# A Strassen feed forward on one Trainium2 core: two sums of weights move from VectorE to GpSimd

## The chip, the cores and the metric

The kernel runs on one core of a Trainium2 chip. The metric is device microseconds of one execution; the comparison is made with the median of several runs. The engines are named as the profile names them: PE (TensorE, matrix products; PEld is its weight load), DVE (VectorE), ACT (ScalarE), POOL (GpSimd) and SP (SyncE, which issues most of the DMAs).

## The reference

The model is one encoder block in fp32 on 256 tokens of width 2048: two branches (a gated linear attention and a Hyena convolution), a merge, a LayerNorm, then the feed forward that this change touches and a second LayerNorm:

```python
h = _layernorm(DEEPNORM_ALPHA * h + mix, ln1_g[l], ln1_b[l])
ff = jnp.square(jax.nn.relu(h @ w_ff1[l])) @ w_ff2[l]      # 2048 -> 8192 -> 2048
h = _layernorm(DEEPNORM_ALPHA * h + ff, ln2_g[l], ln2_b[l])
```

## The kernel before

Every fp32 operand is split into a high and a low part (`cast` on ScalarE makes the high part, `rest` on VectorE subtracts it from the source). A product then takes three matmuls: high by high, high by low, low by high.

The feed forward is worked off in quarters of the 8192 hidden channels. The first quarter of the first matrix (`ff1_first`) runs alone. Then come 48 slots (`ff_pairs`, `SLOTS = 48`). Each slot does two things on TensorE: products of the second matrix for the quarter that is ready, and one block of 128 hidden channels of the first matrix for the next quarter (the f block, lines L147 and L151, summed in one PSUM buffer).

The products with the second matrix use a Strassen scheme (Winograd's form): a weight block of 128 x 2048 is four units a, b, c, d of 128 x 512, and seven products, each a unit or a sum of units by one of seven `forms` of the hidden activations, replace eight. The seven are taken in three parts: units a, b, c as they are (`plain_split`, pieces `b_h` and `b_l`), the two sums a+d and a+b+d (`pair_split`, pieces `whi` and `wlo` from `ring`), and the two sums b+d and a+b+c+d (`last_split`, pieces in `fa`). Their products are on lines L1245, L1246 and L1247 (`form_products`).

The raw block lies in one of three ring buffers (`ring_tile`), which SyncE fills two slots ahead (`ring_load`, L1150). Its four units are u[0] to u[3]. `plain_split` splits a, b, c, then makes the sums in place: u[0] = a+d and u[3] = a+d+b on VectorE. Two DMAs that accumulate, issued by GpSimd, make the others: u[1] = b+d by adding d from memory (L1170), and u[2] = c+a+b+d by adding u[3] (L1171).

Inside a slot the instructions on ScalarE, VectorE and TensorE keep the order in which the program writes them (`pin`, which holds the instruction in program order while `pinned[0]` is set):

1. TensorE: a, b, c of this slot, the two pair products, the f block, then the two last products of the slot before.
2. `plain_split` of the next slot, then the first half of the next f weights (`half_split`, tiles `fraw`).
3. `pair_split` of the next slot; every eighth slot, sums out of PSUM (`take_sums`, tiles `zr`).
4. In the slots that FORMED lists (10, 11, 13, 14, 16, 17, 19, 20 and so on by 16), `forms`: the seven forms of two hidden blocks. In the third round the forms are plain casts with one subtraction.
5. `quad_sum`, which empties the PSUM of the f block into `fr` (ScalarE copies one half to `f_l`, VectorE adds the other); the second half of the f weights; `last_split`. In the last slots, one step of the joins (L1271 to L1278).

Of the kernel before, what the change touches and what calls it, by code (L numbers as in the profile page):

```python
# [13 lines left out]
ALU = mybir.AluOpType  # L14
# [29 lines left out]
def block_kernel(  # L44
# [25 lines left out]
    nc = tc.nc  # L70
# [37 lines left out]
    def weight_half(n, h):  # L108
        return (wp.tile([P, D // 2], F32R, tag="whi", bufs=3, name=f"whi{n}_{h}"),
                wp.tile([P, D // 2], F32R, tag="wlo", bufs=3, name=f"wlo{n}_{h}"))  # L110
# [138 lines left out]
    with tc.tile_pool(name="xp", bufs=1) as xp, tc.tile_pool(name="xq", bufs=1) as xq:  # L249
        def units(pool, tag, n, **kw):  # L250
            t = pool.tile([P, n, OPENING * P], F32R, tag=tag, name=f"open_{tag}", **kw)
            return lambda a, b: t[:, a:b].rearrange("p k (b j) -> p k b j", b=OPENING)
# [41 lines left out]
        for k0, n in PIECES:  # L294
# [13 lines left out]
            if k0 == 0:  # L308
                hi, lo = places[0]
# [775 lines left out]
    def ring_tile(p):  # L1085
        m = p % 3
        if m not in ring:
            ring[m] = wp.tile([P, D], F32, tag="raw", bufs=3, name=f"ring{m}")
        return ring[m]
# [10 lines left out]
    def pin(ins):  # L1100
        return tc.keep_in_program_order(ins) if pinned[0] else ins

    def VT(dst, a, b, op):
        return pin(nc.vector.tensor_tensor(dst, a, b, op=op))  # L1104

    def cast(hi, src):
        return pin(nc.scalar.copy(hi, src))  # L1107

    def rest(lo, src, hi):
        return VT(lo, src, hi.bitcast(F32), ALU.subtract)  # L1110
# [46 lines left out]
    def plain_split(p):  # L1157
        raw, n = ring_tile(p), FF_PAIRS + 2 * p
        hi = ep.tile([P, D], F32R, tag="xh", name=f"b_h{p}")
        lo = ep.tile([P, 1024], F32R, tag="wx", name=f"b_l{p}")  # L1160
        u = units(raw)
        at = slice(0, 1024), slice(1024, 1536)
        low = lo, hi[:, 1536:2048]
        for c in at:
            cast(hi[:, c], raw[:, c])
        for c, dst in zip(at, low):
            rest(dst, raw[:, c], hi[:, c])
        VT(u[0], u[0], u[3], ALU.add)
        VT(u[3], u[0], u[1], ALU.add)
        nc.gpsimd.dma_start(u[1], wblk[n, :, 1536:2048], accum_op=ALU.add)  # L1170
        nc.gpsimd.dma_start(u[2], u[3], accum_op=ALU.add)  # L1171
        h = units(hi)
        pieces_of[p, 0] = list(zip(h[:3], units(lo) + h[3:]))

    def split_units(p, kind, hi, lo, raw):
        by_unit = [t.rearrange("p (u c) -> p u c", c=512) for t in (hi, lo)]
        cast(by_unit[0], raw)
        rest(by_unit[1], raw, by_unit[0])
        pieces_of[p, kind] = list(zip(units(hi), units(lo)))

    def raw_units(p):
        return ring_tile(p).rearrange("p (u c) -> p u c", c=512)

    def pair_split(p):
        hi, lo = weight_half(FF_PAIRS + 2 * p, 0)
        split_units(p, 1, hi, lo, raw_units(p)[:, 0:4:3])

    def last_split(p):
        fa_slot(4)
# [21 lines left out]
    def ff1_first():  # L1211
        begun = begin_three()
        for c2 in range(8):
            for c in range(2):
                if begun:
                    ps, parts, n = begun.pop(0)
                    finish_block(ps, hT, parts, n)
                else:
                    ps = channel_psum(f"f0_{c2}_{c}")
                    parts = next_block()  # L1220
                    for h in range(2):
                        channel_products(ps, hT, parts[h], range(8 * h, 8 * h + 8))
                quad_sum(c2, c, ps, f"f0_{c2}_l{c}")
                at = 2 * c2 + c
                if at in (12, 13):
                    block_load(at - 12)
                if at in (13, 14):
                    ring_load(at - 13)
                if at == 14:
                    plain_split(0)  # L1230
                    pair_split(0)
            sq = squares(c2)
            forms(c2)
            if 2 <= c2 < 6:
                zc = z1[:, 1, (c2 - 2) * 512:(c2 - 1) * 512]
                with tc.issue_after(sq.ins):
                    nc.vector.tensor_tensor(zc, zc, rows1[:, 1, (c2 - 2) * 512:(c2 - 1) * 512], op=ALU.add)
# [43 lines left out]
    def ff_pairs():  # L1281
        pss = [psum_side(f"w{j}") if j not in (2, 3, 4) else psum_main(f"w{j}") for j in range(7)]
        joins = []
        for s in range(SLOTS):
# [12 lines left out]
            if more:  # L1297
                plain_split(s + 1)
                half_split(s + 1, 0)
            take_sums(pss, s, (0, 1, 2))  # L1300
            if more:
                pair_split(s + 1)
# [266 lines left out]
```

## Time and profile before

| | us |
|---|---|
| median of 3 runs | 1796.89 (1796.34 to 1797.45) |
| the profiled execution | 1796.92 |
| its span | 1795.1 |
| PE busy | 1784.6 (99%) |
| DVE busy | 1453.9 (81%) |
| ACT busy | 1037.7 (58%) |
| POOL busy | 164.7 (9%) |

The span is the time between the first and the last event of the profiled execution. The busy time of an engine is the sum of its instructions' spans, without register, semaphore and DMA issuing instructions on most queues; DMA issues of GpSimd do count. The granted clock of TensorE is 1.00 in all windows of the stage. In a row of the timeline stand start, duration, engine, line, operation, output <- inputs, shape and count, and in brackets the idle time of the engine before it with the engine that ended it. VectorE's instructions overlap a little: the next one starts about 0.08 us before the one ahead has ended, so distances of starts are used for sums. The program's helpers `VT` and `rest` record all their instructions at L1104, `cast` at L1107; there one goes by the tile.

### The profile page before, as it was taken

Reading aid. Unit: us, or ns where it says so; the run is one execution under the profiler, and the core shown is the slowest. Engines: PE = TensorE matmul, PEld = TensorE weight load, DVE = VectorE, ACT = ScalarE, POOL = GpSimd, SP = SyncE. Lnnn points to the kernel's source line nnn. Section 1 sums busy time; section 2 is a strip of 40 time slices with the busy share of each in tenths; the row PEclk is TensorE's granted clock in tenths of the full one; section 3 lists DMA queues with packets and bytes.
Section 4 is the critical chain, followed back from the end, with each engine's and each line's share of the span. In section 5 each row is a group of like instructions: output and inputs, shape, how many; then the busy total and the mean of one; then the engine's idle time right before and its main releaser. Section 6 shows DMA issues by size and latency. Waiting matters only on the chain.

```text
span 1795.1 us, 23458 instructions
## 1 busy us (share of the span) xinstructions
PE 1784.6 (99%) x8787; PEld 1506.7 (84%) x8787; DVE 1453.9 (81%) x1869; ACT 1037.7 (58%) x1399; POOL 164.7 (9%) x217
## 2 busy tenths in 40 slices
PE   9999999999999999999999999999999999999998
PEld 7888888888888888888888889888888888888887
DVE  6789887875679998998845558688899999999867
ACT  6678667875344444444544445566666666666632
POOL 1011110000111101111000000001111111111100
PEclk9999999999999999999999999999999999999999
DMA  8668866445797979798555664658888878888763
GB/s 325 233 249 291 253 232 201 144 169 201 235 297 244 287 251 283 246 308 249 203 190 187 266 240 153 225 180 274 250 242 252 271 240 259 255 248 267 216 226 123
DMA packets 79281, 424.76 MB, mean 237 GB/s; under 512 B 9816, under 2 KB 12392, under 8 KB 38464
## 3 DMA queue, kind: packets, MB, share of 16 engines
q1 hardware_dynamic: 47808, 336.61, 50.8%
q0 software_dynamic: 24304, 66.99, 18.2%
q10 hardware_dynamic: 7056, 19.67, 3.1%
q8 instruction: 69, 1.13, 0.3%
q14 instruction: 44, 0.36, 0.1%
HBM read 381.86 MB, written 16.25 MB: 222 GB/s over the span
## 4 chain that ended last, share of the span: by engine, by line
PE 93%; DVE 3%; ACT 1%; DMA 1%; issue 1%; SPq 0%; DVEq 0%; POOL 0%; ACTq 0%
PE f L147 11%; PE f L151 6%; PE w L1246 4%; PE w L1247 4%; PE w L1245 4%; PE g L200 3%; PE g L199 3%; PE g L201 3%; PE ux L199 3%; PE ux L201 3%; PE ux L200 3%; PE k L147 2%; PE v L201 2%; PE v L200 2%; PE v L199 2%; PE ho L200 2%
## 5 line engine op out<-in xcount | busy, mean ns | idle before, releaser
L86 ACT CAST whi<-raw 128x1024 fp32r<-128x1024 f32 x392 | 412.6, 1054 | 408.0 <-PE ux L201 86.8
L87 DVE TENSOR_TENSOR wlo<-raw,whi 128x1024 fp32r<-128x1024 f32 x392 | 477.2, 1221 | 205.1 <-ACT whi L86 202.9
L147 PE MATMUL f<-hT,whi 128*128 128x512 f32 x984 | 242.8, 391 | 1.1 <-DVE fr L1104 1.1
L147 PEld LDWEIGHTS f<-hT,whi 128*128 128x128 f32 x984 | 180.8, 188 | 36.4 <-DVE fr L1104 1.5
L151 PEld LDWEIGHTS f<-hT,wlo 128*128 128x128 f32 x984 | 126.2, 191 | 4.8
L1104 DVE TENSOR_TENSOR wlo<-fraw,whi 128x1024 fp32r<-128x1024 f32 x96 | 117.2, 1220 | 13.3 <-ACT whi L1107 11.0
L151 PE MATMUL f<-hT,wlo 128*128 128x256 f32 x984 | 127.7, 283 | 0.0
L1107 ACT CAST whi<-ring 128x1024 fp32r<-128x1024 f32 x48 | 50.6, 1054 | 102.8 <-DVE ring L1104 98.4
L1170 POOL DMA_DIRECT2D ring<-wblk x48 | 41.7, 868 | 700.9 <-DVE ring L1104 700.9
L1107 ACT CAST whi<-fraw 128x1024 fp32r<-128x1024 f32 x96 | 100.9, 1051 | 0.1
L200 PE MATMUL g<-wlo,xT 128*128 128x512 f32 x256 | 100.2, 391 | 0.0
L201 PE MATMUL ux<-whi,xT 128*128 128x512 f32 x256 | 99.9, 390 | 0.0
L201 PE MATMUL g<-whi,xT 128*128 128x512 f32 x256 | 99.9, 390 | 0.0
L200 PE MATMUL ux<-wlo,xT 128*128 128x512 f32 x256 | 99.7, 389 | 0.0
L199 PE MATMUL g<-whi,xT 128*128 128x512 f32 x256 | 93.9, 392 | 0.0
L199 PE MATMUL ux<-whi,xT 128*128 128x512 f32 x256 | 89.7, 389 | 0.0
L1107 ACT CAST b_h<-ring 128x1024 fp32r<-128x1024 f32 x96 | 75.4, 834 | 22.5 <-PE w L1247 18.0
L1104 DVE TENSOR_TENSOR b_l<-ring,b_h 128x1024 fp32r<-128x1024 f32 x48 | 58.6, 1220 | 12.5 <-ACT b_h L1107 12.5
L1104 DVE TENSOR_TENSOR ring<-ring 128x512 f32<-128x512 f32 x96 | 65.9, 687 | 1.5
L1104 DVE TENSOR_TENSOR wlo<-ring,whi 128x1024 fp32r<-128x1024 f32 x48 | 58.8, 1224 | 1.9 <-ACT whi L1107 0.3
L1104 DVE TENSOR_TENSOR fa<-ring,fa 128x1024 fp32r<-128x1024 f32 x48 | 58.4, 1217 | 0.0
L1171 POOL DMA_DIRECT2D ring<-ring x48 | 58.1, 1210 | 0.0
(537 smaller groups left out, 4297.5 us busy)
## 6 DMA issues: line engine op xcount, KB each, us to landing
raw<-wblk SPq DMA_DIRECT2D x204, 1024.0 KB, 5.1
fraw<-wblk SPq DMA_DIRECT2D x48, 1024.0 KB, 4.8
ring<-wblk SPq DMA_DIRECT2D x48, 1024.0 KB, 7.3
Td<-T POOLq DMA_DIRECT2D x32, 384.0 KB, 5.6
conv_sb<-conv_rows SPq DMA_DIRECT2D x12, 1024.0 KB, 11.6
Tl<-Td POOLq DMA_DIRECT2D x16, 768.0 KB, 9.4
ring<-wblk POOLq DMA_DIRECT2D x48, 256.0 KB, 4.3
ring<-ring POOLq DMA_DIRECT2D x48, 256.0 KB, 5.1
```

What stands on the lines that cost most here:

```text
L86: return (nc.scalar.copy(hi, src), nc.vector.tensor_tensor(lo, src, hi.bitcast(F32), op=ALU.subtract))
L87: nc.vector.tensor_tensor(lo, src, hi.bitcast(F32), op=ALU.subtract))
L147: MM(ps[:, :, ts], hi[:, js], act[:, kt, :, ts], start=(kt == 0 and opens), stop=(kt == KT - 1))
L151: MM(ps[:, 0, ts], lo[:, js], act[:, kt, 0, ts], start=False, stop=False)
L199: MM(pss[tb], sh, wh, start=(kt == 0), stop=False)
L200: MM(pss[tb], sh, wl, start=False, stop=False)
L201: MM(pss[tb], sl, wh, start=False, stop=(kt == KT - 1))
L1104: return pin(nc.vector.tensor_tensor(dst, a, b, op=op))
L1107: return pin(nc.scalar.copy(hi, src))
L1245: pin(MM(ps, sh, wh, start=(i == 0), stop=False))
L1246: MM(ps, sh, wl, start=False, stop=False)
L1247: pin(MM(ps, sl, wh, start=False, stop=(i == 7)))
```

## The change

In `plain_split` both sums go from VectorE to GpSimd, and their places are exchanged: a+d now goes to u[3], and a+d+b to u[0]. The first sum then reads u[0] and u[3] and overwrites u[3], which no other instruction of `plain_split` reads; the second overwrites u[0], and so comes after the cast and the subtraction that read u[0]. The accumulating DMA takes u[0] in place of u[3], and `pair_split` reads the two units in the other order. GpSimd's two sums and its two DMA issues stand in this order in its queue.

```diff
@@ plain_split
         for c, dst in zip(at, low):
             rest(dst, raw[:, c], hi[:, c])
-        VT(u[0], u[0], u[3], ALU.add)
-        VT(u[3], u[0], u[1], ALU.add)
+        pin(nc.gpsimd.tensor_tensor(u[3], u[0], u[3], op=ALU.add))
+        pin(nc.gpsimd.tensor_tensor(u[0], u[3], u[1], op=ALU.add))
         nc.gpsimd.dma_start(u[1], wblk[n, :, 1536:2048], accum_op=ALU.add)
-        nc.gpsimd.dma_start(u[2], u[3], accum_op=ALU.add)
+        nc.gpsimd.dma_start(u[2], u[0], accum_op=ALU.add)
@@ pair_split
-        split_units(p, 1, hi, lo, raw_units(p)[:, 0:4:3])
+        split_units(p, 1, hi, lo, raw_units(p)[:, 3::-3])
```

## The prediction

> **What bounds the kernel now.** I read the page first, then the windows of the stage that the change touches, then what TensorE waits for there, then VectorE's order of work in two kinds of slot.
>
> ```profile
> span 1795.1 us, 23458 instructions
> PE 1784.6 (99%) x8787; PEld 1506.7 (84%) x8787; DVE 1453.9 (81%) x1869; ACT 1037.7 (58%) x1399; POOL 164.7 (9%) x217
> ```
>
> TensorE is busy for all but 10.5 us of the span; VectorE, from which work is taken, is busy for 81% of it. The share is an average, so I look at the stage: the 48 slots of the feed forward, from about 1195 to 1690 us. Window rows give TensorE's, its weight load's, VectorE's, ScalarE's and GpSimd's busy time in turn.
>
> ```profile
> 1190.00:1300.00 110.00, 110.00 (x577) 94.82 (x576) 91.88 (x107) 72.14 (x93) 17.38 (x20) 1.00 0.81 248
> 1300.00:1410.00 110.00, 110.00 (x562) 94.25 (x561) 101.52 (x133) 76.59 (x104) 17.79 (x21) 1.00 0.83 247
> ...
> 1480.00:1590.00 110.00, 108.89 (x562) 93.21 (x561) 103.80 (x138) 71.90 (x97) 17.58 (x20) 1.00 0.81 249
> 1590.00:1690.00 100.00, 99.36 (x506) 84.77 (x505) 90.74 (x107) 64.67 (x84) 17.56 (x20) 1.00 0.84 252
> ```
>
> TensorE has no gap at all in the first two rows and 1.11 and 0.64 us in the last two. The waits of TensorE in the whole stage (1190 to 1700 us; total, times, longest) name both:
>
> ```profile
> PE f L147 <- DVE fr L1104: 1.1, 1, 1.1
> PE w L1246 <- DVE wlo L1104: 0.6, 1, 0.6
> ```
>
> So relief of VectorE can win at most 1.1 + 0.6 = 1.7 us here, 0.1% of the time. About 0.2% (3.6 us) is what a measurement of this kernel can tell from no change. The same windows say how little room there is the other way: VectorE is busy 101.52 of 110 and 103.80 of 110 us in the stretches that hold most of the forms. The chain of waits before the one wait of 1.1 us runs over VectorE, through the sums themselves:
>
> ```profile
> 1546.61 0.60 DVE b_h L1104
> 1547.21 0.61 DVE ring L1104
> ...
> 1553.45 0.35 DVE fr L1104
> 1553.80 0.04 issue
> 1553.84 2.11 PE f L147 x8
> ```
>
> That wait is on `quad_sum`, which empties the one PSUM buffer left for the f block: its VectorE instruction must be through before TensorE opens the next f block.
>
> **The beat of a slot.** TensorE's beat is the distance of two such rows of the chain, 1420.27 - 1409.94 = 10.33 us:
>
> ```profile
> 1409.94 1.91 PE f L151 x16
> 1420.27 1.91 PE f L151 x16
> ```
>
> VectorE in a slot without forms (start, duration, operation, wait before it):
>
> ```profile
> 1232.34 1.22 DVE L1104 TENSOR_TENSOR b_l<-ring,b_h 128x1024 fp32r<-128x1024 f32 x1 [0.77 <-ACT b_h L1107]
> ...
> 1238.64 0.42 DVE L1104 TENSOR_TENSOR fr<-f,f_l 128x256 f32<-128x256 f32 x1 [0.75 <-ACT f_l L1107]
> 1239.59 1.23 DVE L1104 TENSOR_TENSOR wlo<-fraw,whi 128x1024 fp32r<-128x1024 f32 x1 [0.52 <-ACT whi L1107]
> ...
> 1242.71 1.22 DVE L1104 TENSOR_TENSOR b_l<-ring,b_h 128x1024 fp32r<-128x1024 f32 x1 [0.76 <-ACT b_h L1107]
> ```
>
> From b_l to b_l are 10.37 us, of which VectorE waits 0.75 + 0.52 + 0.76 = 2.03, so it needs 8.3 of TensorE's 10.33. A slot with forms:
>
> ```profile
> 1315.48 1.22 DVE L1104 TENSOR_TENSOR b_l<-ring,b_h 128x1024 fp32r<-128x1024 f32 x1
> 1316.62 0.68 DVE L1104 TENSOR_TENSOR b_h<-ring,b_h 128x512 fp32r<-128x512 f32 x1
> 1317.22 1.41 DVE L1104 TENSOR_TENSOR ring<-ring 128x512 f32<-128x512 f32 x2
> 1318.55 1.22 DVE L1104 TENSOR_TENSOR wlo<-fraw,whi 128x1024 fp32r<-128x1024 f32 x1
> ...
> 1322.39 0.69 DVE L1104 TENSOR_TENSOR fa<-fr,fa 128x512 fp32r<-128x512 f32 x1 [0.36 <-ACT fa L1107]
> 1323.00 0.55 DVE L1104 TENSOR_TENSOR fa<-fw,fa 128x384 fp32r<-128x384 f32 x1
> 1323.47 0.41 DVE L1104 TENSOR_TENSOR fr<-f,f_l 128x256 f32<-128x256 f32 x1
> 1324.02 1.23 DVE L1104 TENSOR_TENSOR wlo<-fraw,whi 128x1024 fp32r<-128x1024 f32 x1
> ...
> 1326.30 1.22 DVE L1104 TENSOR_TENSOR b_l<-ring,b_h 128x1024 fp32r<-128x1024 f32 x1
> ```
>
> Here b_l to b_l is 10.82 us, 0.49 over TensorE's beat, with one wait of 0.36. The `fr` instruction ends at 1323.88, and TensorE opens the f block here:
>
> ```profile
> 1325.36 1.07 PE L147 MATMUL f<-hT,whi 128*128 128x512 f32 x4
> ```
>
> So 1325.36 - 1323.88 = 1.5 us is the slack at this deadline. By the list FORMED in the code, full forms stand in slots 10, 11, 13, 14, 16, 17, 19, 20 and again 16 slots later: twice eleven slots with eight forms each. That the books close: the second group has 8 x 0.49 = 3.9 too much, its three other slots give back 3 x 2.03 = 6.1, the seven sums out of PSUM in slots 31 and 32 cost 7 x 0.6 = 4.2 (below, 1528.46 - 1526.66 = 1.8 for three); that leaves 2.0 against a slack of 1.5, and the trace has a wait of 1.1.
>
> ```profile
> 1526.66 1.88 DVE L1104 TENSOR_TENSOR zr<-zr,w 128x512 f32<-128x512 f32 x3
> 1528.46 1.22 DVE L1104 TENSOR_TENSOR wlo<-ring,whi 128x1024 fp32r<-128x1024 f32 x1
> ...
> 1617.23 0.68 DVE L1272 TENSOR_TENSOR zr<-zr 128x512 f32<-128x512 f32 x1
> ...
> 1645.35 0.69 DVE L1104 TENSOR_TENSOR fa<-fr,fa 128x512 fp32r<-128x512 f32 x1 [0.47 <-ACT fa L1107]
> ```
>
> The last two rows are a join (0.68 us, 0.6 start to start, as b_h above: 1317.22 - 1316.62) and one of the four small forms of slots 42 to 46 (0.6 and a wait of 0.47).
>
> **What the change removes.** On VectorE the two sums of each slot, 1318.55 - 1317.22 = 1.33 us start to start. These are the rows for what goes and for what GpSimd does already:
>
> ```profile
> L1104 DVE TENSOR_TENSOR ring<-ring 128x512 f32<-128x512 f32 x96 | 65.9, 687 | 1.5
> L1170 POOL DMA_DIRECT2D ring<-wblk x48 | 41.7, 868 | 700.9 <-DVE ring L1104 700.9
> L1171 POOL DMA_DIRECT2D ring<-ring x48 | 58.1, 1210 | 0.0
> ring<-wblk SPq DMA_DIRECT2D x48, 1024.0 KB, 7.3
> ring<-ring POOLq DMA_DIRECT2D x48, 256.0 KB, 5.1
> ```
>
> If nothing else happened, a forms slot would fall to 9.5 us of VectorE and both waits would go: 1796.9 - 1.7 = 1795.2. TensorE's and SyncE's instruction order stays as it was; ScalarE's and VectorE's differ by a few places in the opening.
>
> **What it adds.** 96 GpSimd instructions on 128x512 fp32. The trace has no arithmetic on GpSimd, so their price is bounded: 0.69 us, the same sum on VectorE, from below; 1.21 us, GpSimd's own longest row on a 128x512 piece of this buffer, is the row of the right engine, and I take it; twice that, 2.42, is my far end. GpSimd itself has room: 2 x 1.21 + 0.87 + 1.21 = 4.5 us of 10.33. In its queue the first sum stands ahead of the second and both ahead of the two DMA issues; the first waits for the raw block (issue to landing 7.3 us), the second for b_l, since it overwrites what b_l reads. Behind the second sum wait the DMAs and ScalarE's cast of the pair. The DMAs have cover: they land after 5.1 us and `last_split` reads them about a slot later. The set-up instruction that GpSimd gets in front of its first sum lies where it is idle, so I cost it at nothing:
>
> ```profile
> 1100.00:1180.00 80.00, 0.00 (x0) 1.00 0.47 171
> ```
>
> [...]
>
> **The open cost: do both engines read at once?** Nearly all VectorE instructions of this stage read two operands in SBUF, as the new sums do. No row shows GpSimd reading SBUF beside VectorE. The ends: no loss at all, or the engines take turns and VectorE loses each sum's whole duration. I take turns as the likelier. With them VectorE's beat changes by 2 x 1.21 - 1.33 = +1.09 us a slot: forms slots need 11.91 (1.58 over the beat), others 9.4 (0.9 under).
>
> - First group: 8 x 1.58 - 3 x 0.9 + 3 x 0.6 (three sums out of PSUM in slots 15 and 16) = 11.7, less slack 1.5: 10.2 us of TensorE waits.
> - Second: 12.6 - 2.7 + 4.2 = 14.1, less 1.5, less the 1.1 there now: 11.5.
> - Slots 39 to 47: nine times 0.9 under is -8.1, seven PSUM sums +4.2, eight joins of 0.6 +4.8, four small forms of about 1.07 +4.3: 5.2, less 1.5, less the 0.6 there now: 3.1.
>
> That is 24.8. In a forms slot GpSimd can run below the `fr` instruction (one operand from PSUM; 1324.02 - 1323.47 = 0.55 to the next start) and the wait of 0.36; taking 0.35 of that as used, 16 x 0.35 = 5.6 come off: +19.2 us, so 1796.92 + 19.2 = 1816. The profiled execution took 1796.92 us (span 1795.1), the median of the runs is 1796.89, so nothing needs correcting.
>
> [...]
>
> **Rivals.**
> 1. Side by side. Both engines run at full rate, VectorE falls to 9.5 us in forms slots, the second sum is ready 1.21 us after b_l, sooner than VectorE's two were (b_h lay between). The two waits go: 1795.2 us. For it: GpSimd is busy 17.38 of 110 us in the first window. Against it: nothing in the rows. It decides if VectorE's 1.22 us subtractions keep their duration.
> 2. GpSimd sets the beat. At 2.42 us a sum and turns, VectorE gains 3.51 a slot: forms slots 14.3 (4.0 over, 16 times: 64), the others 11.8 (1.5 over, 31 times: 46): about 1907 us. It needs the far end of the price.
> 3. Turns lost. The second sum finds VectorE already in the subtraction behind b_h and starts 1.14 us later (the distance of two 128x1024 starts, 1316.62 - 1315.48); ScalarE's cast of the pair and VectorE's next subtraction wait for it. In the 16 forms slots that is 18 us more, 1834; in the eight join slots too, 1843.
>
> **How the numbers follow.** Turns, with rival 3 as their upper part: 0.64, of which 0.04 ends within 0.2% because the sums cost nearer 0.69 (2 x 0.69 - 1.33 is 0.05, which changes nothing). Side by side: 0.28, of which 0.26 is no measurable change, since 1.7 us is under 3.6, and 0.02 a larger gain elsewhere. GpSimd as the bound: 0.06. Something that I don't see and that speeds it up: 0.02. The chance for turns is a judgement on an operation without a row; what the rows fix is that there is nearly nothing to win and that the forms slots have no room to lose. Range: from side by side (1795) to turns lost in all loaded slots (1843); the likeliest case alone is 1800 to 1843. Faster 0.04, same 0.30, slower 0.66.
>
> **What would show it.** If turns: VectorE's 1.22 us rows grow in some executions to about 2.4 or show idle time that GpSimd releases, and TensorE's waits at the f block (on `fr`) sum to some 20 us, in slots 10 to 20 and 26 to 36 and hardly elsewhere. If GpSimd's rows are near 1.2 us, the price holds; near 2.4, rival 2. If VectorE's durations don't move and its busy time falls by 66 us, side by side is right and the forecast is wrong. Waits of ScalarE's pair cast on GpSimd well over the 2.08 us that it waits for VectorE now would be rival 3:
>
> ```profile
> 1401.09 1.05 ACT L1107 CAST whi<-ring 128x1024 fp32r<-128x1024 f32 x1 [2.08 <-DVE ring L1104]
> ```

## The result, and the profile after

The change makes the kernel slower: 1810.99 us (median of 6 runs, 1809.1 to 1812.78) against 1797.12 us (1796.34 to 1797.45), a ratio of 1.0079 with a 95% interval of 1.0069 to 1.0089. The forecast was 1816 us, slower. The profiled execution is the fastest of the six: 1809.1 us, with a span of 1807.3 us, 12.2 us over that of before. From the page of the changed kernel:

```profile
span 1807.3 us, 23439 instructions
PE 1789.6 (99%) x8787; PEld 1506.7 (83%) x8787; DVE 1477.6 (82%) x1773; ACT 1038.5 (57%) x1399; POOL 321.4 (18%) x313
```

VectorE has 96 instructions fewer and yet 23.7 us more busy time (1477.6 after, 1453.9 before). The groups of the changed kernel say which instructions grew (count, busy time in all, mean ns of one, idle time before them):

```profile
L1104 DVE TENSOR_TENSOR wlo<-fraw,whi 128x1024 fp32r<-128x1024 f32 x96 | 176.9, 1843 | 11.0 <-ACT whi L1107 9.6
L1168 POOL TENSOR_TENSOR ring<-ring 128x512 f32<-128x512 f32 x48 | 77.3, 1611 | 371.0 <-DMA ring<-wblk 363.4
L1169 POOL TENSOR_TENSOR ring<-ring 128x512 f32<-128x512 f32 x48 | 80.2, 1671 | 168.9 <-DVE b_l L1104 168.9
```

VectorE's subtraction `wlo<-fraw` took 1220 ns on average before and takes 1843 now; its operands and shape are the same. VectorE's order in the forms slot that the prediction showed, one slot from b_l to b_l:

```profile
1317.10 1.21 DVE L1104 TENSOR_TENSOR b_l<-ring,b_h 128x1024 fp32r<-128x1024 f32 x1
1318.23 0.68 DVE L1104 TENSOR_TENSOR b_h<-ring,b_h 128x512 fp32r<-128x512 f32 x1
1318.83 2.31 DVE L1104 TENSOR_TENSOR wlo<-fraw,whi 128x1024 fp32r<-128x1024 f32 x1
1321.18 1.23 DVE L1104 TENSOR_TENSOR wlo<-ring,whi 128x1024 fp32r<-128x1024 f32 x1
...
1324.84 0.42 DVE L1104 TENSOR_TENSOR fr<-f,f_l 128x256 f32<-128x256 f32 x1
1325.39 1.77 DVE L1104 TENSOR_TENSOR wlo<-fraw,whi 128x1024 fp32r<-128x1024 f32 x1
...
1328.22 1.21 DVE L1104 TENSOR_TENSOR b_l<-ring,b_h 128x1024 fp32r<-128x1024 f32 x1
```

and GpSimd's two sums in the same slot (the bracket is its idle time and what ended it):

```profile
1318.44 1.62 POOL L1169 TENSOR_TENSOR ring<-ring 128x512 f32<-128x512 f32 x1 [3.49 <-DVE b_l L1104]
...
1324.46 1.61 POOL L1168 TENSOR_TENSOR ring<-ring 128x512 f32<-128x512 f32 x1 [2.33 <-DMA ring<-wblk]
```

Read the two together. GpSimd's second sum is released by b_l at 1318.44, while VectorE is in b_h; b_h ends at 1318.91, the sum at 1320.06. VectorE's next subtraction is in its row from 1318.83, but it ends at 1321.14, 1.08 us after the sum, and has taken 2.31 - 1.22 = 1.09 us more than before. The first sum begins at 1324.46 and lies in part beside `fr`, which reads one operand from PSUM and keeps its 0.42 us; the next subtraction takes 1.77 - 1.22 = 0.55 us more. VectorE's slot is now 1328.22 - 1317.10 = 11.12 us; it was 10.82, and TensorE's beat is 10.33. This slot is one of the mildest. The fourteen forms slots in which no sum out of PSUM falls take 11.10 to 12.64 us from b_l to b_l, 11.48 on average; before they took 10.80 to 10.82. Into the two longest, 12.53 and 12.64 us, falls the cost of two first sums.

The windows of the stage (those shown of before) and what TensorE and its weight load wait for in it (total, times, longest):

```profile
1190.00:1300.00 110.00, 109.45 (x572) 94.05 (x572) 96.43 (x87) 72.13 (x94) 48.98 (x38) 1.00 0.80 245
1300.00:1410.00 110.00, 107.46 (x547) 91.20 (x546) 104.08 (x108) 71.60 (x98) 51.13 (x42) 1.00 0.80 242
...
1480.00:1590.00 110.00, 105.27 (x527) 88.74 (x526) 104.43 (x113) 69.27 (x94) 48.41 (x40) 0.98 0.78 235
1590.00:1690.00 100.00, 99.48 (x504) 84.07 (x503) 91.62 (x92) 64.18 (x84) 51.11 (x40) 1.00 0.86 265
```

```profile
PE f L147 <- DVE fr L1104: 6.7, 5, 2.3
PE w L1245 <- DVE zr L1104: 1.1, 2, 0.6
PE w L1246 <- DVE wlo L1104: 1.0, 2, 0.5
```

```profile
PEld f L147 <- DVE fr L1104: 9.8, 8, 2.8
PEld w L1246 <- DVE wlo L1104: 2.5, 4, 1.0
PEld w L1245 <- issue: 1.0, 1, 1.0
PEld w L1245 <- ACT f_l L1107: 0.9, 1, 0.9
```

TensorE's gaps now stand mainly where the forms are. Its weight load waits 14.2 us in all. Before, the same answer for the weight load had two rows, 2.6 us:

```profile
PEld f L147 <- DVE fr L1104: 1.5, 1, 1.5
PEld w L1246 <- DVE wlo L1104: 1.1, 1, 1.1
```

The difference, 11.6 us, is nearly the span's 12.2; the lists of the matmuls alone would have shown 7.1. The ends of matmuls are modelled in this profile, and the other 5.0 us of the span stand in PE's busy time (1784.6 before, 1789.6 after). Where the time goes, slot by slot, comes from the chain, which has a row for TensorE's low products in many slots. Before:

```profile
1296.35 1.91 PE f L151 x16
...
1502.88 1.91 PE f L151 x16
...
1566.28 1.91 PE f L151 x16
...
1639.50 1.91 PE f L151 x16
```

and after, with the row that answers to 1409.94 of before:

```profile
1297.62 1.91 PE f L151 x16
...
1415.36 1.90 PE f L151 x16
...
1508.35 1.91 PE f L151 x16
...
1577.94 1.91 PE f L151 x16
...
1651.64 1.91 PE f L151 x16
```

The lag is 1.27 us at the first pair of rows, 5.42 at the second, 5.47 at the third, 11.66 at the fourth and 12.14 at the last: 4.15 us come in over the first group of forms slots, 6.19 over the second, 0.05 between them, 0.48 from there to the end. The fourth pair of rows stands ahead of the last two forms slots of the second group; 0.31 of the 0.48 come in there (the row of the low products at 1586.77 before, 1598.74 after).

### The profile page after: what moved, and what is told of

The parts are those of the page before. It is cut to its first block, busy times and chain, and to the rows that moved or that the text cites. A ratio compares the mean times of both kernels' runs of the same rounds, so it can differ in the third digit from the quotient of the medians.

```text
span 1807.3 us, 23439 instructions
## 1 busy us (share of the span) xinstructions
PE 1789.6 (99%) x8787; PEld 1506.7 (83%) x8787; DVE 1477.6 (82%) x1773; ACT 1038.5 (57%) x1399; POOL 321.4 (18%) x313
## 4 chain that ended last, share of the span: by engine, by line
PE 89%; DVE 5%; ACT 2%; issue 2%; POOL 1%; DMA 1%; DVEq 0%; SPq 0%; ACTq 0%; POOLq 0%
PE f L147 10%; PE f L151 5%; PE g L200 3%; PE g L199 3%; PE g L201 3%; PE ux L199 3%; PE ux L200 3%; PE ux L201 3%; PE w L1246 3%; PE w L1247 3%; PE w L1245 3%; PE r L199 2%; PE r L201 2%; PE r L200 2%; PE k L147 2%
## 5 line engine op out<-in xcount | busy, mean ns | idle before, releaser
L1104 DVE TENSOR_TENSOR wlo<-fraw,whi 128x1024 fp32r<-128x1024 f32 x96 | 176.9, 1843 | 11.0 <-ACT whi L1107 9.6
L1168 POOL TENSOR_TENSOR ring<-ring 128x512 f32<-128x512 f32 x48 | 77.3, 1611 | 371.0 <-DMA ring<-wblk 363.4
L1169 POOL TENSOR_TENSOR ring<-ring 128x512 f32<-128x512 f32 x48 | 80.2, 1671 | 168.9 <-DVE b_l L1104 168.9
L1104 DVE TENSOR_TENSOR b_l<-ring,b_h 128x1024 fp32r<-128x1024 f32 x48 | 63.2, 1317 | 5.8 <-ACT b_h L1107 5.6
L1104 DVE TENSOR_TENSOR fa<-ring,fa 128x1024 fp32r<-128x1024 f32 x48 | 67.1, 1397 | 0.0
L466 POOL DMA_DIRECT2D Td<-T x32 | 19.2, 605 | 213.1 <-DVE T L462 212.6
## 6 DMA issues: line engine op xcount, KB each, us to landing
conv_sb<-conv_rows SPq DMA_DIRECT2D x12, 1024.0 KB, 11.6
```

The source lines that it names most:

```text
L1168: pin(nc.gpsimd.tensor_tensor(u[3], u[0], u[3], op=ALU.add))
L1169: pin(nc.gpsimd.tensor_tensor(u[0], u[3], u[1], op=ALU.add))
```

## The experiments

Two theories at first, both drawn from these rows. Turns: where a VectorE instruction with two SBUF operands and a GpSimd sum meet, one gets on only when the other has ended, as the rows of 2.31 and 1.77 us suggest, and VectorE loses the time in which they overlap. Late pair: VectorE's durations don't matter; the loss is that ScalarE's cast of the pair now waits for a sum of 1.67 us on GpSimd (the mean of L1169), which took 0.69 on VectorE.

**Four more GpSimd sums behind each slot of the kernel before**, on a scratch tile of 128x256 (it is made and filled once ahead of the slots; those two lines are left out here):

```diff
         nc.gpsimd.dma_start(u[2], u[3], accum_op=ALU.add)
+        for _ in range(4):
+            pin(nc.gpsimd.tensor_tensor(scr, scr, scr, op=ALU.add))
```

> The kernel before, VectorE's two sums kept, with four more GpSimd sums of 128x256 on a scratch tile behind the second DMA issue of every slot; nothing waits for them and no engine's order changes. Turns (VectorE instructions with two SBUF operands and GpSimd sums exclude each other): GpSimd holds the operands some 2.6 us a slot, VectorE keeps its 1.33 us of sums, so forms slots need about 12.5 us or more against a beat of 10.33: 1815 to 1850 us, with VectorE rows grown beyond 1.22 us. Late pair (the loss is only that the pair's cast waits for the second sum on GpSimd): nothing waits, so 1797 us and VectorE's durations unchanged.

Measured: 1826.87 us, ratio 1.0169 (1.0156 to 1.0183). No instruction in the slots waits for these sums, and both sums of the pair are VectorE's here, so the late pair can't explain it. The group of the sums, and one of the VectorE rows that they stretch (minimum, median, maximum):

```profile
L1175 POOL TENSOR_TENSOR scr<-scr 128x256 f32<-128x256 f32 x192 | 218.1, 1136 | 11.4
```

```profile
L1104 DVE TENSOR_TENSOR wlo<-ring,whi x48: 1209/1625/1669, 1195.1 to 1714.6; 128x1024 fp32r<-128x1024 f32 x48
```

The median subtraction of the pair grows from 1.226 to 1.625 us.

**Eight fills in their place**, which write the same tile and read nothing:

```diff
+        for _ in range(8):
+            pin(nc.gpsimd.memset(scr, 0.0))
```

> As the extra sums, with eight GpSimd fills (memset) of the 128x256 scratch tile in their place: GpSimd is busy and writes SBUF but reads nothing. Turns over operands that are read: 1797 us, VectorE's rows stay at 1.22 us. If any GpSimd work blocks VectorE: a loss as with the extra sums, in the measure of the fills' busy time. Late pair: 1797 us.

Measured: 1797.19 us, ratio 1.0004 (0.9995 to 1.0013).

```profile
L1175 POOL MEMSET scr<- 128x256 f32 x384 | 152.3, 396 | 19.4
```

```profile
L1104 DVE TENSOR_TENSOR wlo<-fraw,whi x96: 1211/1220/1227, 1197.1 to 1686.1; 128x1024 fp32r<-128x1024 f32 x96
```

GpSimd is busy for 152.3 us with them, 3.2 us a slot, and no VectorE row moves: the longest of these subtractions takes 1.227 us, as before. So neither GpSimd's being busy nor its writing stretches VectorE's rows here; the sums differ from the fills in that they also read.

**The sums left out** of the changed kernel, which then adds up something else than the reference. What is the relief of VectorE worth at most?

```diff
-        pin(nc.gpsimd.tensor_tensor(u[3], u[0], u[3], op=ALU.add))
-        pin(nc.gpsimd.tensor_tensor(u[0], u[3], u[1], op=ALU.add))
```

> The change with both sums left out, on either engine (the two pieces of the pair are then the plain units a and d, and the DMA adds a): the most that relief of VectorE by 1.33 us a slot can bring. Turns and late pair alike: both waits of TensorE go, 1795 us, 0.1% under the kernel before. Should VectorE's relief be worth more than TensorE's idle time says: below 1793 us.

Measured: 1794.04 us, ratio 0.9987 (0.9978 to 0.9996), and TensorE has no wait left in the stage. So even sums at no cost on any engine win 0.1%; no arrangement of them can win more.

**One sum of the two on GpSimd.** First the first one alone (the second becomes `VT(u[0], u[3], u[1], ALU.add)`):

> The change with its second sum (a+b+d) back on VectorE; only the first is on GpSimd. Turns: a forms slot loses 0.55 us (first sum mostly under instructions that read PSUM) to 1.1 us and saves 0.66: 1796 to 1801 us. Late pair: the second sum is VectorE's again, so 1796 us.

Measured: 1798.38 us, ratio 1.0007 (0.9998 to 1.0017), not told from the kernel before. Then the second alone, again an edit of the changed kernel:

```diff
-        pin(nc.gpsimd.tensor_tensor(u[3], u[0], u[3], op=ALU.add))
+        VT(u[3], u[0], u[3], ALU.add)
         pin(nc.gpsimd.tensor_tensor(u[0], u[3], u[1], op=ALU.add))
```

> The change with its first sum (a+d) back on VectorE; only the second is on GpSimd. Turns: a forms slot loses 1.09 us to the second sum (2.31 for 1.22 us) and saves one sum of 0.66, so it needs about 11.25 us: 1798 to 1805 us. Late pair: the second sum is still GpSimd's and the pair's cast still waits for it, so the whole loss stays: 1809 to 1813 us.

Measured: 1832.42 us, ratio 1.02 (1.0186 to 1.0214). Both theories missed: one sum on GpSimd costs more than two. The timeline of this kernel, VectorE first, then GpSimd:

```profile
1318.18 0.68 DVE L1104 TENSOR_TENSOR ring<-ring 128x512 f32<-128x512 f32 x1
1318.78 1.22 DVE L1104 TENSOR_TENSOR wlo<-fraw,whi 128x1024 fp32r<-128x1024 f32 x1
1322.26 1.23 DVE L1104 TENSOR_TENSOR wlo<-ring,whi 128x1024 fp32r<-128x1024 f32 x1 [2.26 <-ACT whi L1107]
```

```profile
1319.00 2.14 POOL L1169 TENSOR_TENSOR ring<-ring 128x512 f32<-128x512 f32 x1 [8.11 <-DVE ring L1104]
```

Now VectorE's own first sum releases GpSimd's at 1319.00, and VectorE went into the subtraction at 1318.78. The subtraction keeps its 1.22 us; the GpSimd sum takes 2.14, and then VectorE is idle for 2.26 us until ScalarE has cast the pair. The sums of 46 of the 48 slots take over 2 us, and VectorE waits 101.0 us in the stage for casts of this kind, where it waited 11.3 before. That is the prediction's rival 3, turns lost, in a kernel that was meant to halve the loss. A third theory, from these two timelines: who comes first gets the turn. In the change the sum was released 0.39 us ahead of VectorE's subtraction (1318.44 against 1318.83), and VectorE paid 1.09 us; here the subtraction is 0.22 us ahead of the sum, and VectorE pays the wait for sum and cast, 2.26 us.

**The turn given back**: the same, with VectorE's first sum ahead of b_l, so that b_l releases the second sum while b_h runs.

```diff
+        VT(u[3], u[0], u[3], ALU.add)
         for c, dst in zip(at, low):
             rest(dst, raw[:, c], hi[:, c])
-        VT(u[3], u[0], u[3], ALU.add)
         pin(nc.gpsimd.tensor_tensor(u[0], u[3], u[1], op=ALU.add))
```

> Second sum on GpSimd as in the run that had it alone there, but VectorE's first sum is put ahead of b_l instead of behind b_h, so that the second sum is released while b_h still runs. Whoever comes first gets the turn (theory now): GpSimd gets it as in the change, VectorE pays 1.09 us on the next subtraction but no longer waits 2.26 us for the pair's cast; a forms slot needs 11.12 - 0.55 + 0.60 = 11.2 us, as in the change: 1807 to 1814 us. If the second sum on GpSimd costs what it did there whoever comes first (late pair): 1828 to 1834 us.

Measured: 1813.13 us, ratio 1.0089 (1.0074 to 1.0104). VectorE and GpSimd:

```profile
1327.72 0.69 DVE L1104 TENSOR_TENSOR b_h<-ring,b_h 128x512 fp32r<-128x512 f32 x1
1328.32 2.32 DVE L1104 TENSOR_TENSOR wlo<-fraw,whi 128x1024 fp32r<-128x1024 f32 x1
1330.68 1.23 DVE L1104 TENSOR_TENSOR wlo<-ring,whi 128x1024 fp32r<-128x1024 f32 x1
```

```profile
1327.89 1.67 POOL L1169 TENSOR_TENSOR ring<-ring 128x512 f32<-128x512 f32 x1 [7.45 <-DVE b_l L1104]
```

The same instructions on the same engines, one of them moved by two places, and 19 us come back: the subtraction is long again (2.32) and VectorE's wait for the cast is gone.

Two things moved at once, though: the sum is there before the subtraction (1327.89 against 1328.32), and it is also released earlier. Slots of this run in which GpSimd lost the turn all the same tell the two apart. There are eight among the 48, with sums of 2.80 us or more; in each the sum was released as early as in the others. The one among them that is a forms slot without sums out of PSUM takes 12.31 us from b_l to b_l, as such slots do in the run before (12.30); where GpSimd got the turn they take 11.18 to 11.20. So it is the turn that counts, 1.1 us a forms slot, and not the earlier release. It also corrects the third theory: in all eight the sum had been released 0.43 or 0.44 us before VectorE's next instruction began, and that one still went first. Coming first did not win the turn in these eight slots of 48; what decided there, no run shows.

That the total comes out beside the change's 1811 is in part chance. In the profiled execution 5.7 us of the loss come in at one place behind the forms slots (by 1667 us), where VectorE waits 3.28 us for a raw block, a term that the expectation did not have.

**Which slots pay.** Two runs chose the engine for each sum by the slot in which it runs:

```diff
-        pin(nc.gpsimd.tensor_tensor(u[3], u[0], u[3], op=ALU.add))
-        pin(nc.gpsimd.tensor_tensor(u[0], u[3], u[1], op=ALU.add))
+        heavy = [FORMED.get(s, 0) >= 8 for s in (p - 2, p - 1)]
+        ADD = nc.vector.tensor_tensor, nc.gpsimd.tensor_tensor
+        pin(ADD[not heavy[0]](u[3], u[0], u[3], op=ALU.add))
+        pin(ADD[not heavy[1]](u[0], u[3], u[1], op=ALU.add))
```

and the same without `not`. (The list FORMED counts the small forms too: 20 slots, not 16.)

> GpSimd makes a sum only where it runs in a slot without forms; the sums that run in slots with full forms are on VectorE. Turns: the slots without forms have 0.9 us of room or more, so nothing or little is lost: 1796 to 1800 us. Late pair: two thirds of the second sums are GpSimd's, so two thirds of the 14 us stay: 1804 to 1808 us.

> The reverse: GpSimd makes a sum only where it runs in a slot with full forms, 16 of 48; VectorE makes the others. Turns: the loss lies in these slots, so most of it stays: 1804 to 1811 us. Late pair: a third of the 14 us stays: 1800 to 1803 us.

Measured: 1803.73 us (ratio 1.0034, 1.0021 to 1.0047) and 1817.63 us (1.0113, 1.0098 to 1.0128). Both missed upward, and together they lose 28 us where the change loses 14. Their mixed blocks have a first sum on VectorE ahead of a second on GpSimd: VectorE's sum releases GpSimd's in 9 of 28 and in 10 of 20 cases, with sums of up to 2.15 us, the picture of the turn lost. As a test of the place they are spoilt. Two more runs keep both sums of a block on one engine (on GpSimd if neither, or if either, of the two slots is in the list):

> Both sums of a block on GpSimd or both on VectorE, so that no first sum on VectorE stands ahead of a second on GpSimd: on GpSimd for the 19 blocks whose sums run in no slot of the list FORMED. Turns: these slots have room, 1796 to 1800 us. Late pair: 19 of 48 second sums, two fifths of 14 us: 1801 to 1803 us.

> The other 29 blocks: both sums on GpSimd where one of them runs in a slot of FORMED, on VectorE elsewhere. Turns: nearly all of the change's loss lies there: 1806 to 1813 us. Late pair: three fifths of 14 us: 1804 to 1806 us.

Measured: 1799.53 us (ratio 1.0012, 1.0002 to 1.0022) for 19 blocks, 1806.67 us (1.0055, 1.004 to 1.007) for 29. The sum, 3.0 + 10.2 = 13.2 us over the kernel before, is the change's 13.9; 77% of it lies with the blocks at the forms. The light blocks agree with turns and not with the late pair; the heavy ones (1805.25 to 1808.63) agree with turns and lie just above the late pair.

No version that makes both sums beats the kernel before, and the run without sums says that none can by more than 0.1%.

## Why the prediction was right

The direction, the cause and the place of most of the loss were right; the size was 19 us where the median has 13.9 and the profiled execution 12.2.

- The bound. TensorE has no room to win: the forecast's 1.7 us stand against 2.3 us of the kernel without sums, 0.1% either way.
- Turns. Shown by the extra sums against the extra fills, and by VectorE's rows: 1.22 to 2.31 us beside a GpSimd sum, 1.22 beside a fill, and 0.42 as before for `fr` with its PSUM operand. The rows of the changed kernel divide in the same way: with both operands in SBUF `wlo<-fraw` reaches 2.342 us and `b_l` 2.322, with one in PSUM `fr` takes at most 0.426 and `zr<-zr,w` 0.687. The delay shows on either engine: the subtraction ends 1.08 us after the sum beside it (1321.14 against 1320.06), and in the run with the second sum alone on GpSimd the sum ends 1.14 us after the subtraction beside it (1321.14 against 1320.00). Before these runs turns were the author's judgement, without a row.
- The late pair costs the change next to nothing. Over the stage VectorE waits for the casts of its subtractions as long as before (first line before, second after; total, times, longest), and the one wait of 2.3 us belongs to the one lost turn below:

```profile
DVE wlo L1104 <- ACT whi L1107: 11.3, 23, 0.5
DVE wlo L1104 <- ACT whi L1107: 11.9, 21, 2.3
```

- The price, 1.21 us, was close, by luck in part: the row that it was taken from is a DMA issue, not a sum. A first sum in a gap of VectorE, which has only `fr` between 1239.16 and 1240.81:

```profile
1239.06 1.28 POOL L1168 TENSOR_TENSOR ring<-ring 128x512 f32<-128x512 f32 x1 [0.19 <-DMA ring<-wblk]
```

  The means of the two sums, 1.61 and 1.67 us, hold the wait for the turn; behind b_h, 1320.06 - 1318.91 = 1.15 us remain. The set-up instruction, costed at nothing, shows as two rows of 0.04 us at 899.1 (MODIFY_POOL_CONFIG, L1168), after which GpSimd is idle until 1181.88.
- What a sum costs VectorE. The forecast charged the whole of both sums. Measured is less, as only part of a sum overlaps an instruction with two SBUF operands: in the slot shown 1.09 us for the second and 0.55 for the first, 1.64 in place of 2.42. Over the whole kernel VectorE's busy time rose by 23.7 us although 65.9 us of sums left it, so it paid 89.6 us for 96 sums, 0.93 each. The forecast's cover of 0.35 us a forms slot, the author's estimate, was too small and its price a little low, and the two errors nearly cancel: it had 11.91 - 0.35 = 11.56 us for a forms slot and 9.4 for one without, and measured are 11.48 and, in the four slots between forms slots without sums out of PSUM, 9.37.
- The mis-sized term is what those slots add up to in a group. For eight forms slots and three others, VectorE was forecast to need 11.7 and 14.1 us, less 2.8 for cover, over eleven beats: 8.9 and 11.3. From b_l to b_l it took 120.59 and 122.71 us against 11 x 10.33 = 113.63: 7.0 and 9.1. The sums out of PSUM were charged 0.6 us each on top; the slots without forms that hold two or three of them lose a wait of about 0.75 us that the others keep, so part of that work costs nothing. The prediction's check of its books had such slots give back 2.03 us each before the change; between forms slots they gave back 1.0 to 1.3 (9.00 to 9.31 us, without sums out of PSUM), because some 0.75 us of that wait stays even when VectorE is behind, so that the books closed by chance.
- By the groups, less 2.8 each for cover: 7.4 forecast and 4.15 measured; 8.7 and 6.5 (6.19 + 0.31); 3.1 and under 0.2 behind them, where nine slots were forecast to bring VectorE 5.2 us over the beat. Why the joins cost so little is not taken apart here. Not forecast: 0.84 us in the first slots, where VectorE still makes forms of the opening (b_l to b_l 10.67 us from 1203.57, 9.05 before). The rest of the 1.27 at 1296, 0.43, stood already before the stage (1196.24 against 1195.81 for the same row).
- Not in the sum at all: the granted clock. The longest wait of TensorE, 2.34 us, is followed by matmuls at a lower clock (window: busy, count, clock, DMA share and GB/s; then the 16 low products, which take 2.08 otherwise):

```profile
1560.00:1570.00 10.00, 7.66 (x35) 0.83 0.69 187
```

```profile
1566.37 3.14 PE L151 MATMUL f<-hT,wlo 128*128 128x256 f32 x16
```

- Rival 1, side by side, is excluded: 1795.2 us was its time. Rival 2 too: the sums of over 2 us in this kernel, ten of 96, all start beside a VectorE instruction of two operands. Rival 3 happened in one slot of 48: a second sum of 3.96 us, from 1631.00, behind which VectorE waits 2.27 us for the cast. It happened throughout at 1832 us, where VectorE's own sum releases GpSimd's. That 1832 lies near the 1834 worked out for rival 3 is luck: the 1834 has two sums on GpSimd and the delay in 16 slots, the run one sum and the delay in nearly all.
- The six runs of the change scatter by 3.7 us, the six of before beside them by 1.1; but other series of the kernel before scatter by 2.3 to 3.5 us, so a larger scatter of the change is not shown.

## What to carry to other kernels

Moving an instruction from a busy engine to an idle one can cost the busy one more than it saves: here each sum saved VectorE 0.66 us and cost it 0.93 on average, and the busy total of the relieved engine rose from 1453.9 to 1477.6 us. First ask what the relief is worth at best; a run that leaves the work out tells it (0.1% here). Where rows of one engine grow beside rows of another, as VectorE's here from 1.22 to 2.31 us, compare not only durations but which of the two comes first: one instruction moved by two places was worth 19 us. And judge a price by many slots: the one slot shown has a loss of 0.30 us where the average is 0.67.

## What the runs showed that was not expected

- A GpSimd sum that lost the turn took 2.14 us, against 1.28 alone, and held up ScalarE's cast and with it VectorE's next subtraction, by 2.26 us, so that one sum on GpSimd (1832.42 us) is worse than two (1810.99 us).
- A gap of 2.34 us on TensorE was followed by a granted clock of 0.83 over the ten microseconds around it; the 16 low products behind it took 1.06 us longer. The length of the gap alone does not decide: in the run with the second sum alone on GpSimd a gap of 1.76 us was followed by 0.83 too, and in the run with GpSimd's sums in the slots of FORMED one of 2.40 us left the clock at 1.00. What else does, no run shows.
- GpSimd did not always get the turn when it came first: in eight slots of 48 of the run at 1813.13 us a VectorE instruction that began 0.43 or 0.44 us after the sum was released went ahead of it.
